# Moving four groups of on-chip tiles to 96 bytes past a multiple of 128

## The chip, the cores and the metric

The kernel runs on one core of a Trainium2 chip. The metric is the time of one execution on the device in microseconds; a kernel's time is the median of its runs. TensorE (PE) multiplies matrices out of the on-chip memory SBUF into PSUM, VectorE (DVE), ScalarE (ACT) and GpSimd (POOL) work on elements, SyncE (SP) issues most transfers. SBUF has 128 partitions; a tile takes the same range of bytes in each of them, and its place is the first byte of that range.

## The reference

One inference step of a streaming encoder of two layers, in float32, for 512 new frames of one prompt and 16 frames of each of 8 running streams, 640 frames in all, with a width of 1024:

```python
# layer 0: convolution module, then feed-forward
a, gate = jnp.split(rms_norm(h, g) @ w_pw1 + b_pw1, 2, axis=-1)
glu = a * jax.nn.sigmoid(gate)
y = depthwise_conv(concat(hist, glu), w_dw) + b_dw          # width 31
h = h + jax.nn.silu(layer_norm(y, ln_g, ln_b)) @ w_pw2 + b_pw2
a, b = jnp.split(rms_norm(h, g) @ w_in, 2, axis=-1)          # 1024 -> 2 x 2816
h = h + (jax.nn.silu(a) * b) @ w_out
# layer 1: shared K and V, attention with 16 heads of 64, then feed-forward
k, v = jnp.split(rms_norm(h, norm_kv) @ w_kv, 2, axis=-1)
q = rms_norm(h, norm_attn) @ w_q
h = h + softmax(q @ k.T / 8 + bias) @ v @ w_o                # banded, own cache per stream
h = swiglu_ffn(h, ...)
return rms_norm(h, norm_final), conv buffers, k, v
```

## The kernel before

Activations stand with features on the partitions: a tile holds 128 features, 8 tiles make the width. The 640 frames are the columns, in two groups: group 0 has 256 (all sample frames and the first 128 of the prompt), group 1 has 384 (`GR`).

Every large product is made of three, since an operand is split into a high and a low half that TensorE takes in the type fp32r: `mm3` (lines 157 to 162) issues, for each tile of 128 features, high weights by high activations (L160), low weights by high activations (L161) and high weights by low activations (L162). Each matmul loads its own 128 x 128 stationary tile first (a PEld row of the profile) and then streams 256 or 384 columns. The activations' halves are the tiles `xh` and `xl` (of group 0 and of group 1), the hidden layer of the feed-forward network has both halves in one tile `hid` per group, and the attention output has `ohi` and `olo`. In the V projection the roles are swapped: xh and xl are stationary and the weights stream.

Weights come from memory as `raw`, 1 MB at a time at most (`wsplit`, L124 and L129); ScalarE makes the high half `whi` (L140), VectorE and GpSimd the low half `wlo` (L144). Each of the three has two buffers.

The order of the work is layer 0's convolution module, with group 0 ahead of group 1 by a written plan (`PLAN`); three chunks of layer 0's feed-forward network for group 0 (6 of 22 hidden tiles each), run while VectorE still convolves group 1; the remaining chunk of 4 for both groups; three chunks of 6 for group 1; the attention of 8 pairs of heads, with the projections of the next pair between; and layer 1's feed-forward network for both groups in chunks of 9, 9 and 4. In a chunk, `ffn_in` makes one hidden tile per step (48 matmuls per group: two halves of the gate, 8 tiles, 3 products), and `out_tile` then adds the chunk's share to each of 8 output tiles (3 products for each hidden tile of the chunk: 18, 12 or 27 matmuls). A scheduler places the instructions of each engine in the program by a simulated timeline; SBUF tiles are placed by pools: constants first (`cst`), then the weights (`wp`), then temporary pools, each tile behind the one allocated before it.

So a tile's place follows from the sizes of all tiles ahead of it. `i4` (L341 of the kernel before) is a constant of 128 bytes right ahead of `xh` and `xl`; `t256s` (L578) is the last constant ahead of the weights; `bt` (L596) stands right ahead of `ohi` and `olo`; `KK` (L706) comes behind these.

Of the kernel before, what the change touches and what calls it, by code (L numbers as in the profile page):

```python
# [8 lines left out]
F32 = mybir.dt.float32  # L9
F32R = mybir.dt.float32r  # L10
# [4 lines left out]
P = 128  # L15
# [5 lines left out]
NP = H // 2  # L21
# [19 lines left out]
F1 = ((0, 9), (9, 9), (18, 4))  # L41
FP = (8, 4)
CM = 6
# [11 lines left out]
SSQ = 'avavavav'  # L55
SCUT = 8
CB, QB, KB = 5, 1, 1
OG = (0, 1)
BO = "a0 s0 a1 s1 b0 b1 t0 p0 c0 t1 c1"
BL = "a0 s0 a1 s1 t0 b0 b1 c0 t1 c1 p0"  # L60
FG = (1, 0)
# [10 lines left out]
def tile_trunk(ctx, tc, xT, vecs, hist, w_pw1, w_pw2, w_in0, w_out0, w_in1, w_out1,  # L72
# [3 lines left out]
    cst = ctx.enter_context(tc.tile_pool(name="cst", bufs=1))  # L76
# [8 lines left out]
    def nm(s):  # L85
        uid[0] += 1
        return f"{s}_{uid[0]}"
# [4 lines left out]
    def w2t():  # L92
        return w2.tile([P, 1024], F32, tag="w2", name=nm("w2"))
# [164 lines left out]
    def ffn_in(wsrc, j, xs, hid, jj, groups, pool):  # L258
        wh, wl = wsplit(wsrc[j], 16, P, pool=pool)
        for g in groups:  # L260
            n = GR[g][1]
            ps = []
            for ab in range(2):
                pt = mmt()
                mm3(pt[:, :n], [(wh[:, (ab * 8 + k) * P:(ab * 8 + k + 1) * P],
                                 wl[:, (ab * 8 + k) * P:(ab * 8 + k + 1) * P]) for k in range(KT)],
                    xk(xs[g], range(KT)))
                ps.append(pt[:, :n])
            bc = xs[g][2]
            with tc.high_priority(offset=HP):  # L270
                s = tp.tile([P, 384], F32, tag="t1", name=nm("t1"))
                t = tp.tile([P, 384], F32, tag="t2", name=nm("t2"))
                if bc is None:
                    nc.scalar.activation(out=s[:, :n], in_=ps[0], func=AF.Silu)
                    nc.vector.tensor_tensor(out=t[:, :n], in0=s[:, :n], in1=ps[1], op=ALU.mult)
                else:
                    nc.vector.tensor_tensor(out=s[:, :n], in0=ps[0], in1=bc, op=ALU.mult)  # L277
                    nc.scalar.activation(out=s[:, :n], in_=s[:, :n], func=AF.Silu)  # L278
                    nc.vector.tensor_tensor(out=t[:, :n], in0=ps[1], in1=bc, op=ALU.mult)  # L279
                    nc.vector.tensor_tensor(out=t[:, :n], in0=s[:, :n], in1=t[:, :n], op=ALU.mult)  # L280
                xsplit(t[:, :n], hid[g][0][:, jj, :], hid[g][1][:, jj, :])
# [23 lines left out]
                for m in range(KT):  # L305
                    out_tile(ws[m // mg], ch, (m % mg) * ch, m, g, hid)

    def ffn(pool, w_in, w_out, xs, groups, chunks, pl=0, og=None, cm=CM):
        for j0, ch in chunks:
            hid = {}  # L310
            for g in groups:
                n = GR[g][1]
                t = pool[g].tile([P, 2 * cm * n], F32, tag=f"hid{g}", name=nm("hid"))
                t = t.bitcast(F32R).rearrange("p (s k n) -> p s k n", s=2, k=cm)
                hid[g] = t[:, 0], t[:, 1]
            for jj in range(ch):
                ffn_in(w_in, j0 + jj, xs, hid, jj, groups, pl)
            ffn_out(w_out, j0, ch, hid, og or groups, pl)
# [19 lines left out]
    nc.gpsimd.memset(gs[:, :, 9, 0:14], 0.0)  # L338
    gp = cp.tile([P, KT, GPW], F32, name="gp", tag="gp")
    nc.gpsimd.memset(gp[:, :, HIST + 384:], 0.0)  # L340
    i4 = cst.tile([P, 32], F32, name="i4", tag="i4")  # L341
    nc.gpsimd.tensor_tensor(out=i4, in0=ident[:, 0:32], in1=ident[:, 32:64], op=ALU.add)
    for b in range(2, 4):
        nc.gpsimd.tensor_tensor(out=i4, in0=i4, in1=ident[:, 32 * b:32 * b + 32], op=ALU.add)
# [5 lines left out]
    with tc.high_priority(offset=2 * HP):  # L350
        xs = [rms(0, V_NCONV, SSQ, SCUT, nc.vector), None]
# [151 lines left out]
    chunks = list(FS)  # L503
# [43 lines left out]
    if FC:  # L547
        ffn({0: hp0, 1: hp1}, w_in0, w_out0, {0: xs0, 1: xs1}, (0, 1), FC)
# [4 lines left out]
    xs = [rms_late(0, None), rms_late(1, None)]  # L553
# [9 lines left out]
    ap = at.enter_context(tc.tile_pool(name="ap", bufs=1))  # L563
# [11 lines left out]
    BS = ap.tile([P, 576], F32, name="BS", tag="BS")  # L575
    nc.gpsimd.memset(BS[:, 0:384], 0.0)
    nc.gpsimd.memset(BS[:, 512:576], NEG)
    ts_ = cst.tile([P, NP], F32, name="t256s", tag="t256s")  # L578
    for b in range(4):
        for hh in range(2):  # L580
            r0 = b * 32 + hh * 16
# [2 lines left out]
                                      ap=[[0, 16], [2 * L, NP]]))  # L584

    def bias_load(p):
        for hh in range(2):
            hd = 2 * p + hh
            nc.sync.dma_start(BP[:, hh, 256:512],
                              bass.AP(tensor=rel.tensor, offset=rel.offset + hd * L + 127,  # L590
                                      ap=[[RELW - 1, P], [1, 256]]))
            nc.gpsimd.tensor_scalar(out=BP[:, hh, 256:512], in0=BP[:, hh, 256:512],
                                    scalar1=t256[:, hd:hd + 1], scalar2=8.0,
                                    op0=ALU.subtract, op1=ALU.mult)
            nc.gpsimd.memset(BP[0:64, hh, 448:512], NEG)
        bt = ap.tile([P, 160], F32, tag="bt", name=nm("bt"), bufs=1)  # L596
        for b in range(4):
            nc.sync.dma_start(bt[b * 32:(b + 1) * 32, 0:128],
                              bass.AP(tensor=rel.tensor, offset=rel.offset + 2 * p * L + 127,
                                      ap=[[L, 2], [RELW - 1, 16], [1, 128]]))  # L600
            nc.sync.dma_start(bt[b * 32:(b + 1) * 32, 128:144],
                              bass.AP(tensor=rel.tensor, offset=rel.offset + 2 * p * L + 255,
                                      ap=[[L, 2], [RELW - 1, 16], [1, 16]]))
        nc.gpsimd.tensor_scalar(out=BS[:, 384:512], in0=bt[:, 0:128], scalar1=ts_[:, p:p + 1],
                                scalar2=8.0, op0=ALU.subtract, op1=ALU.mult)
        for b in range(4):
            nc.gpsimd.tensor_scalar(out=BS[b * 32:(b + 1) * 32, 512 + b * 16:528 + b * 16],
                                    in0=bt[b * 32:(b + 1) * 32, 128:144],
                                    scalar1=ts_[b * 32:(b + 1) * 32, p:p + 1],
                                    scalar2=8.0, op0=ALU.subtract, op1=ALU.mult)  # L610
# [72 lines left out]
    def proj_o(r):  # L683
        wh, wl = wsplit(w_o[r], 16, P)
        for g in OG if r == NP // 2 - 1 else (0, 1):
            g0, n = GR[g]
# [10 lines left out]
    def head_a(p, hh):  # L697
        kt, qt = kts[p], qts[p]
        r = slice(hh * DH, hh * DH + DH)
        S = sp.tile([P, 1280], F32, tag="S", name=nm("S"))  # L700
        mx = ap.tile([P, 4], F32, tag="mx", name=nm("mx"), bufs=3)
        sm = ap.tile([P, 4], F32, tag="sm", name=nm("sm"), bufs=3)
        wide = w2t()
        st = w2t()
        ro = slice(DH - hh * DH, 2 * DH - hh * DH)
        KK = ap.tile([P, 512], F32R, tag="KK", name=nm("KK"), bufs=KB)  # L706
        KL = ap.tile([P, 512], F32R, tag="KL", name=nm("KL"), bufs=KB)
        QQ = ap.tile([P, 512], F32R, tag="QQ", name=nm("QQ"), bufs=KB)
        nc.scalar.activation(out=KK[r], in_=kt[r, P:], func=AF.Copy)
        nc.scalar.activation(out=QQ[r], in_=qt[r, P:], func=AF.Copy)  # L710
        nc.gpsimd.tensor_copy(KK[ro], KK[r].bitcast(F32))
        for to in (r, ro):
            nc.vector.tensor_tensor(out=KL[to], in0=kt[r, P:], in1=KK[r].bitcast(F32),
                                    op=ALU.subtract)
        nc.vector.tensor_tensor(out=QQ[ro], in0=qt[r, P:], in1=QQ[r].bitcast(F32),
                                op=ALU.subtract)
        pss = []
        for i in ORD:
            n = (i + 1) * P
            o = SOFF[i]  # L720
            q = slice(i * P, (i + 1) * P)
            ps = st[:, 640:896] if i == 1 else wide[:, o:o + n]
            nc.tensor.matmul(ps, QQ[:, q], KK[:, 0:n], start=True, stop=False)  # L723
            nc.tensor.matmul(ps, QQ[:, q], KL[:, 0:n], start=False, stop=True)
            pss.append(ps)
        for ii, i in enumerate(ORD):
            n = (i + 1) * P
            o = SOFF[i]
            addmax(S[:, o:o + n], pss[ii], BP[:, hh, 512 - n:512], mx[:, ii:ii + 1])
        rs = softmax_rows(S, mx, sm, [(SOFF[i], (i + 1) * P) for i in ORD])  # L730
        for ii, i in enumerate(ORD):
            n = (i + 1) * P
            o = SOFF[i]
            nc.vector.tensor_scalar(out=S[:, o:o + n], in0=S[:, o:o + n],
                                    scalar1=rs[:, ii:ii + 1], scalar2=None, op0=ALU.mult)
        return S, st
# [128 lines left out]
    tp = hf.enter_context(tc.tile_pool(name="tp1", bufs=2))  # L865
    hpf = hf.enter_context(tc.tile_pool(name="hpf1", bufs=1))
    xs = {g: rms_late(g, V_NFFN + KT) for g in FG}
    ffn({0: hpf, 1: hpf}, w_in1, w_out1, xs, FG, F1, 0, (1, 0), max(ch for _, ch in F1))
    bcs = {}
    with tc.high_priority(offset=HP):  # L870
        for g in (1, 0):
# [4 lines left out]
    for g in (1, 0):  # L876
        g0, n = GR[g]
# [95 lines left out]
```

## Time and profile before

| | us |
|---|---|
| median of 3 runs | 1594.21 |
| lowest and highest run | 1593.93, 1598.01 |
| span of the profiled execution, first to last instruction | 1590.2 |
| TensorE busy in it | 1519.2 |
| VectorE busy in it | 969.4 |
| ScalarE busy in it | 604.7 |
| GpSimd busy in it | 398.0 |

The profiled execution has no time of its own beside its span; the median of the runs is 4.0 us above that span, which is what lies ahead of the first and behind the last instruction, and the difference between executions.

In the profile's rows a line such as L160 is a line of the kernel, an arrow points from the operands to the result, and "128x384" is the shape that streams. A matmul's duration runs until its result is out, and the next begins long before that, so the distance between two starts is what a matmul costs the span. The clock that TensorE was granted was full in nearly all of the span (mean 0.990).

### The profile page before, as it was taken

The numbers are of one execution on the slowest core, as the hardware profiler recorded it, in microseconds if no ns is written. First come the engines' busy times: TensorE is split into PE (matmuls) and PEld (weight loads), VectorE is DVE, ScalarE is ACT, GpSimd is POOL, SyncE is SP. The second block draws the span as 40 slices with busy tenths as digits, with TensorE's granted clock in tenths as the row PEclk, the third lists the DMA queues.
The fourth block names the chain that finished last, engine by engine and source line by source line (L and its number), as shares of the span: only waits on it lengthen the run. The fifth ranks groups of instructions, "written<-read, shape, count | busy, mean of one in ns | idle before, by whom it ended". The sixth has DMA issues, their size and how long they took to land.

```text
span 1590.2 us, 26820 instructions
## 1 busy us (share of the span) xinstructions
PE 1519.2 (96%) x10998; PEld 1450.4 (91%) x10998; DVE 969.4 (61%) x1781; ACT 604.7 (38%) x1064; POOL 398.0 (25%) x368
## 2 busy tenths in 40 slices
PE   5988998989999999999999999998999999999997
PEld 5868898889999999999987898986999999999997
DVE  5995999988535545446776668577544334433335
ACT  4544454535423323234654345443422112221222
POOL 6854577877401000004221111012100000000001
PEclk9999999999999999999999999999999999999999
DMA  7884345444321343434555454451121232112311
GB/s 240 234 221 135 124 127 166 133 160 159 133 80 59 115 146 102 136 113 139 211 180 171 168 191 160 159 169 52 56 80 45 60 121 80 56 43 76 107 54 67
DMA packets 58700, 199.98 MB, mean 126 GB/s; under 512 B 10193, under 2 KB 22737, under 8 KB 45777
## 3 DMA queue, kind: packets, MB, share of 16 engines
q1 hardware_dynamic: 58288, 197.96, 38.5%
q8 instruction: 86, 1.41, 0.4%
q10 hardware_dynamic: 288, 0.31, 0.1%
q14 instruction: 38, 0.30, 0.1%
HBM read 187.02 MB, written 11.22 MB: 125 GB/s over the span
## 4 chain that ended last, share of the span: by engine, by line
PE 74%; DVE 15%; issue 3%; POOL 3%; DMA 3%; ACT 2%; SPq 0%; POOLq 0%; ACTq 0%; DVEq 0%
PE mm L160 22%; PE mm L162 22%; PE mm L161 22%; DVE w L424 5%; DVE wlo L144 4%; DVE xl L150 2%; PE w L779 1%; PE am L764 1%; PE am L747 1%; PE am L810 1%; ACT whi L140 1%; DVE hid L150 1%; DMA x<-sc 1%; POOL wlo L144 1%; PE w L723 1%
## 5 line engine op out<-in xcount | busy, mean ns | idle before, releaser
L161 PE MATMUL mm<-xh,wlo 128*128 128x256 f32 (+1 forms) x2048 | 638.8, 313 | 13.1 <-DVE wlo L144 12.5
L160 PE MATMUL mm<-xh,whi 128*128 128x256 f32 (+1 forms) x2048 | 635.9, 314 | 7.9 <-ACT xh L149 3.6
L162 PE MATMUL mm<-xl,whi 128*128 128x256 f32 (+1 forms) x2048 | 634.8, 312 | 0.3
L161 PEld LDWEIGHTS mm<-xh,wlo 128*128 128x128 f32 x2048 | 387.9, 190 | 16.6 <-DVE wlo L144 15.6
L160 PEld LDWEIGHTS mm<-xh,whi 128*128 128x128 f32 x2048 | 385.9, 190 | 13.1 <-ACT xh L149 6.7
L162 PEld LDWEIGHTS mm<-xl,whi 128*128 128x128 f32 x2048 | 387.1, 190 | 2.5 <-DVE xl L150 1.4
L140 ACT ACTIVATE whi<-raw 128x2048 fp32r<-128x2048 f32 (+3 forms) x140 | 235.0, 1682 | 340.3 <-PE mm L162 284.0
L144 DVE TENSOR_TENSOR wlo<-raw,whi 128x2048 fp32r<-128x2048 f32 (+6 forms) x140 | 259.7, 1857 | 77.9 <-ACT whi L140 76.3
L161 PE MATMUL mm<-hid,wlo 128*128 128x384 f32 (+1 forms) x704 | 217.3, 310 | 6.6 <-DVE wlo L144 6.6
L162 PE MATMUL mm<-hid,whi 128*128 128x384 f32 (+1 forms) x704 | 215.1, 309 | 0.0
L160 PE MATMUL mm<-hid,whi 128*128 128x384 f32 (+1 forms) x704 | 213.8, 309 | 0.0
L144 POOL TENSOR_TENSOR wlo<-raw,whi 128x1536 fp32r<-128x1536 f32 (+3 forms) x50 | 145.1, 2905 | 69.5 <-ACT whi L140 68.6
L279 DVE TENSOR_TENSOR t<-mm,bc 128x384 f32<-128x384 f32 x66 | 33.8, 512 | 194.5 <-PE mm L162 194.5
L161 PEld LDWEIGHTS mm<-hid,wlo 128*128 128x128 f32 x704 | 132.3, 188 | 8.0 <-DVE wlo L144 8.0
L162 PEld LDWEIGHTS mm<-hid,whi 128*128 128x128 f32 x704 | 131.9, 188 | 0.4 <-DVE hid L150 0.3
L160 PEld LDWEIGHTS mm<-hid,whi 128*128 128x128 f32 x704 | 131.4, 188 | 0.3 <-ACT hid L149 0.2
L217 POOL TENSOR_TENSOR rst<-rst,mhalf 128x2 f32<-128x2 f32 (+1 forms) x7 | 6.0, 863 | 460.2 <-DVE rst L213 460.2
L290 DVE TENSOR_TENSOR h<-mm,h 128x384 f32<-128x384 f32 (+1 forms) x112 | 53.9, 486 | 107.3 <-PE mm L162 107.2
L424 DVE SCALAR_TENSOR_TENSOR w<-gp,dwv,w 128x384 f32<-128x384 f32 x180 | 103.9, 611 | 0.8
L278 ACT ACTIVATE t<-t 128x384 f32<-128x384 f32 x66 | 32.3, 489 | 162.3 <-DVE t L277 162.3
L149 ACT ACTIVATE hid<-t 128x384 fp32r<-128x384 f32 (+1 forms) x88 | 40.6, 462 | 119.1 <-DVE t L280 85.4
L183 POOL TENSOR_TENSOR acc<-sq,sq 128x384 f32<-128x384 f32 (+1 forms) x9 | 9.2, 1023 | 265.2 <-ACT sq L167 265.1
(154 smaller groups left out, 1897.3 us busy)
## 6 DMA issues: line engine op xcount, KB each, us to landing
raw<-in_w_in SPq DMA_DIRECT2D x62, 1024.0 KB
raw<-in_w_pw SPq DMA_DIRECT2D x22, 1024.0 KB
raw<-in_w_out SPq DMA_DIRECT2D x24, 768.0 KB
cache<-in_ck SPq DMA_DIRECT2D x32, 512.0 KB
cache<-in_cv SPq DMA_DIRECT2D x32, 512.0 KB
raw<-in_w_out SPq DMA_DIRECT2D x16, 576.0 KB
raw<-in_w_kq SPq DMA_DIRECT2D x8, 1024.0 KB
x<-sc SPq DMA_DIRECT2D x16, 368.0 KB
```

The lines of the kernel that those rows point to most:

```text
L140: nc.scalar.activation(out=hi[:, a:b], in_=raw[:, a:b], func=AF.Copy)
L144: eng.tensor_tensor(out=lo[:, a:b], in0=raw[:, a:b], in1=hi[:, a:b].bitcast(F32), op=ALU.subtract)
L149: nc.scalar.activation(out=hi, in_=src, func=AF.Copy)
L150: nc.vector.tensor_tensor(out=lo, in0=src, in1=hi.bitcast(F32), op=ALU.subtract)
L160: nc.tensor.matmul(ps, wh, xh, start=(i == 0), stop=False)
L161: nc.tensor.matmul(ps, wl, xh, start=False, stop=False)
L162: nc.tensor.matmul(ps, wh, xl, start=False, stop=(i == last))
L278: nc.scalar.activation(out=s[:, :n], in_=s[:, :n], func=AF.Silu)
L279: nc.vector.tensor_tensor(out=t[:, :n], in0=ps[1], in1=bc, op=ALU.mult)
L290: nc.vector.tensor_tensor(out=hp(g, m), in0=pt[:, :n], in1=hp(g, m), op=ALU.add)
L424: nc.vector.scalar_tensor_tensor(out=dst, in0=src, scalar=wj, in1=dst, op0=ALU.mult, op1=ALU.add)
L723: nc.tensor.matmul(ps, QQ[:, q], KK[:, 0:n], start=True, stop=False)
```

## The change

Four constants are added, and five places use them. Tiles are made larger than what is used of them, so that what is allocated behind them, or the used part itself, moves:

- `i4` gets 24 more float32 (96 bytes) behind it: all later constants move by 96 bytes, xh and xl of both groups among them.
- `t256s` gets 8 more (32 bytes): with the 96 this makes 128, so that weights and all later tiles move by 128.
- `bt` gets 16 more (64 bytes): `ohi` and `olo` and what lies behind them move by 192 in all.
- `KK` gets 16 more ahead of its used part, which brings it and what is behind it to 256.
- Layer 1's hidden tile of group 1 gets 16 more ahead of its used part.

The two built programs give these places, as bytes past a multiple of 128 (in brackets the place modulo 512):

| tile | before | after |
|---|---|---|
| xh, xl (group 0 and group 1) | 0 (256) | 96 (352) |
| raw, whi, wlo (both buffers) | 32 (416) | 32 (32) |
| hid of layer 0, both groups | 96 (96) | 96 (224) |
| hid of layer 1, group 0 | 32 (32) | 32 (160) |
| hid of layer 1, group 1 | 32 (32) | 96 (224) |
| ohi, olo (pairs 0 to 6) | 32 | 96 |
| KK, KL, QQ | 96 | 96 |
| the factors bc of group 1, of group 0 | 32, 64 | 0, 32 |

All rows inside these tiles have lengths that are multiples of 128 bytes. The instructions, their order on every engine and their waits are the same in both programs.

```diff
+XPAD, WPAD, OPAD, HPAD = 24, 8, 16, 16
...
-    def ffn(pool, w_in, w_out, xs, groups, chunks, pl=0, og=None, cm=CM):
+    def ffn(pool, w_in, w_out, xs, groups, chunks, pl=0, og=None, cm=CM, pad=(0, 0)):
...
-                t = pool[g].tile([P, 2 * cm * n], F32, tag=f"hid{g}", name=nm("hid"))
-                t = t.bitcast(F32R).rearrange("p (s k n) -> p s k n", s=2, k=cm)
+                t = pool[g].tile([P, pad[g] + 2 * cm * n], F32, tag=f"hid{g}", name=nm("hid"))
+                t = t[:, pad[g]:].bitcast(F32R).rearrange("p (s k n) -> p s k n", s=2, k=cm)
...
-    i4 = cst.tile([P, 32], F32, name="i4", tag="i4")
+    i4 = cst.tile([P, 32 + XPAD], F32, name="i4", tag="i4")[:, 0:32]
...
-    ts_ = cst.tile([P, NP], F32, name="t256s", tag="t256s")
+    ts_ = cst.tile([P, NP + WPAD], F32, name="t256s", tag="t256s")[:, 0:NP]
...
-        bt = ap.tile([P, 160], F32, tag="bt", name=nm("bt"), bufs=1)
+        bt = ap.tile([P, 160 + OPAD], F32, tag="bt", name=nm("bt"), bufs=1)
...
-        KK = ap.tile([P, 512], F32R, tag="KK", name=nm("KK"), bufs=KB)
+        KK = ap.tile([P, OPAD + 512], F32R, tag="KK", name=nm("KK"), bufs=KB)[:, OPAD:]
...
-    ffn({0: hpf, 1: hpf}, w_in1, w_out1, xs, FG, F1, 0, (1, 0), max(ch for _, ch in F1))
+    ffn({0: hpf, 1: hpf}, w_in1, w_out1, xs, FG, F1, 0, (1, 0), max(ch for _, ch in F1), (0, HPAD))
```

## The prediction

> **What bounds the kernel now.** I read the page's head and its first part, then the busy time by stage, then the waits of TensorE, and last single matmuls in the timeline, since the change alters nothing but where tiles lie. TensorE first:
>
> ```profile
> span 1590.2 us, 26820 instructions
> PE 1519.2 (96%) x10998; PEld 1450.4 (91%) x10998; DVE 969.4 (61%) x1781; ACT 604.7 (38%) x1064; POOL 398.0 (25%) x368
> ```
>
> The share hides two regimes. By stage (TensorE alone, columns: window, its length, busy time and instructions, granted clock, DMA share, GB/s):
>
> ```profile
> 0.00:389.00 389.00, 339.07 (x2652) 0.97 0.55 170
> 389.00:757.00 368.00, 366.57 (x2218) 1.00 0.36 116
> 757.00:1116.00 359.00, 348.98 (x2986) 1.00 0.48 160
> 1116.00:1577.00 461.00, 461.00 (x3128) 1.00 0.21 67
> ```
>
> From 389 us TensorE is idle for 1.4 us, then 10.0, then 0.0: whatever shortens its stream there shortens the span. Before 389 us it loses 50 us. The last such stretch, the first feed-forward chunks of group 0, with all engines, and its one cause of waiting:
>
> ```profile
> 206.00:389.00 183.00, 165.15 (x1324) 160.22 (x1324) 170.84 (x256) 91.71 (x122) 147.97 (x74) 0.98 0.46 150
> ...
> PE mm L161 <- DVE wlo L144: 17.5, 15, 3.6
> ```
>
> VectorE (fourth group of figures) is busy 170.84 of 183 us and TensorE waits 17.5 us for its low halves of the weights; a quicker matmul there mostly waits longer.
>
> What a matmul costs is its start-to-start time, the **pace**, not its duration, since they overlap. These rows of the timeline are the first matmuls of stretches that have no gap:
>
> ```profile
> 638.26 0.34 PE L160 MATMUL mm<-hid,whi 128*128 128x384 f32 x1
> ...
> 663.22 0.34 PE L160 MATMUL mm<-xh,whi 128*128 128x384 f32 x1
> ...
> 714.10 0.34 PE L160 MATMUL mm<-hid,whi 128*128 128x384 f32 x1
> ...
> 1549.00 0.34 PE L160 MATMUL mm<-hid,whi 128*128 128x384 f32 x1
> ...
> 1565.90 0.28 PE L160 MATMUL mm<-hid,whi 128*128 128x256 f32 x1
> ```
>
> From 638.26 to 663.22 us run 8 output tiles of 6 x 3 matmuls of layer 0: 24.96 us / 144 = **173.3 ns**. From 663.22 to 714.10 run 6 weight steps of 48 on xh and xl: 50.88 / 288 = **176.7**. From 1549.00 to 1565.90 run 8 x 4 x 3 of layer 1: 16.90 / 96 = **176.0**. Engine, shape and operation are the same, and the runs are long. What differs is the place. By the built programs (the table ahead) the weights lie 32 bytes past a multiple of 128 throughout; layer 0's hid lies at 96 (64 from the weights), layer 1's at 32 (0 from them), xh and xl at 0. The same for 256 columns:
>
> ```profile
> 369.91 0.28 PE L160 MATMUL mm<-hid,whi 128*128 128x256 f32 x1
> ...
> 373.32 0.39 PE L160 MATMUL mm<-hid,whi 128*128 128x256 f32 x2
> ...
> 482.29 0.28 PE L160 MATMUL mm<-hid,whi 128*128 128x256 f32 x1
> ...
> 493.60 0.34 PE L160 MATMUL mm<-hid,whi 128*128 128x384 f32 x1
> ...
> 510.37 0.33 PE L160 MATMUL mm<-xh,whi 128*128 128x384 f32 x1
> ...
> 1145.44 0.28 PE L160 MATMUL mm<-xh,whi 128*128 128x256 f32 x1
> ...
> 1151.20 0.34 PE L160 MATMUL mm<-xh,whi 128*128 128x384 f32 x1
> ```
>
> hid at 96: 30 matmuls from 369.91 to 373.32 are **113.7 ns** each, 96 from 482.29 to 493.60 are **117.8**; xh at 0, 48 from 1145.44 to 1151.20: **120.0**. And 96 of 384 columns from 493.60 to 510.37: **174.7**. So a place at 96 has a faster and a slower pattern, and each observed one is faster than xh. One stretch of layer 0 (561 to 587 us, 144 matmuls), interrupted by small matmuls, is worse:
>
> ```profile
> L162 PE MATMUL mm<-hid,whi 128*128 128x384 f32 x20 | 6.8, 338 | 0.0
> ...
> L160 PE MATMUL mm<-hid,whi 128*128 128x384 f32 x43 | 13.9, 335 | 0.0
> ```
>
> Its mean duration is 338 ns (first row, 576 to 586 us) against 335 in the fast stretch (second row, 640 to 662 us). Durations move with the pace, so I take 173.3 + 3 = 176.3 ns for all of it, a little pessimistic for its start.
>
> **The change part by part.** No instruction is added, removed or reordered on any engine. xh and xl of both groups go from 0 to 96, layer 1's hid of group 1 from 32 to 96, the attention outputs from 32 to 96; weights stay at 32, layer 0's hid at 96, and layer 1's hid of group 0 at 32. The counts after 389 us:
>
> ```profile
> L161 PE MATMUL mm<-xh,wlo 128*128 128x384 f32 x896 | 303.7, 339 | 0.0
> ...
> L161 PE MATMUL mm<-xh,wlo 128*128 128x256 f32 x544 | 153.7, 283 | 0.0
> ...
> L162 PE MATMUL mm<-wlo,xh 128*128 128x256 f32 x160 | 45.3, 283 | 0.0
> ...
> L161 PE MATMUL mm<-ohi,wlo 128*128 128x384 f32 x64 | 21.6, 337 | 0.0
> ...
> L161 PE MATMUL mm<-ohi,wlo 128*128 128x256 f32 x64 | 18.1, 284 | 0.0
> ...
> L160 PE MATMUL mm<-hid,whi 128*128 128x384 f32 x176 | 59.5, 338 | 0.0
> ```
>
> Each row is one of three products, so there are 2688 matmuls of 384 columns and 1632 of 256 on xh and xl, 480 of the V projection (weights moving, xh stationary), 192 and 192 on the attention output, and 528 on layer 1's hid of group 1 (last row, from 1100 us on).
>
> The new pace is the mean of what the trace shows at 96. 384 columns: (288 x 173.3 + 96 x 174.7 + 144 x 176.3) / 528 = **174.4**. 256 columns: three chunks like 113.7 and one like 117.8 give **114.7**.
>
> - xh and xl, 384: 2688 x (176.7 - 174.4) = 6.2 us (at best x 3.4 = 9.1, at worst x 0.4 = 1.1).
> - xh and xl, 256: 1632 x (120.0 - 114.7) = 8.6 (x 6.3 = 10.3; x 2.2 = 3.6).
> - layer 1's hid, 384: 528 x (176.0 - 174.4) = 0.8 (1.4; 0).
> - attention output: durations 337 and 284 are those of layer 1's hid and of xh, so 192 x 1.6 + 192 x 5.3 = 1.3 (1.7; 0.4).
> - V projection: moving and stationary swap roles; the two go from 32 apart to 64 apart. No row shows that pair at 64. Between nothing and 480 x (120.0 - 114.7) = 2.5 I take 0.7, nearer nothing, as its duration (283) is that of xh.
> - before 389 us: 1440 matmuls of 256 and 384 of 384 would give 1440 x 6.3 + 384 x 3.4 = 10.4 at best, nothing if VectorE decides throughout. I take 1.0, since VectorE does in the stretch above.
>
> Sum: 6.2 + 8.6 + 0.8 + 1.3 + 0.7 + 1.0 = 18.6 us. The span becomes 1590.2 - 18.6 = 1571.6; the median of the runs, 1594.21, lies 4.0 us above the span before, which gives **1576 us**.
>
> Other engines touch the moved tiles too:
>
> ```profile
> L149 ACT ACTIVATE hid<-t 128x384 fp32r<-128x384 f32 x19 | 9.6, 507 | 0.0
> ...
> L149 ACT ACTIVATE hid<-t 128x384 fp32r<-128x384 f32 x22 | 11.6, 525 | 85.4 <-DVE t L280 85.4
> ```
>
> ScalarE's write of hid takes 507 ns in layer 0 (at 96) and 525 in layer 1 (at 32): 18 ns either way, under 14 us of TensorE work per step of both groups. I cost it at nothing; uncovered, 22 writes would be 0.4 us. Nothing that feeds TensorE becomes late: from 1116 to 1577 us it never waits, and its steps would shorten by some 3% only.
>
> A rule of the Trainium skill speaks against all this. "TensorE: Matmul & The Clock Gate", section "Step-by-step: what each phase is for", says that the moving operand and the weights come through two independent read ports, so that loading the next weights takes no bandwidth from the running matmul. By that rule a tile's place would have no price. The rows of 335 against 339 ns for the same form at the same clock do not fit, unless something other than the place makes them.
>
> **The rivals.**
>
> - *Nothing changes.* The paces come from what ran before a stretch, not from the place. For it: hid at the same place ran with 335 and with 338. Against it: 96 matmuls of layer 1's hid in one run stayed at 176.0, and xh, entered from everything, stays at 120.0 and 176.7. Time 1594.
> - *The slower pattern takes over.* Every tile at 96 settles at 117.8 and 176.3: 1.1 + 3.6 + 0 + 0.4 = 5.1 us, 1589. For it: once in a pattern a stretch keeps it. Against it: half of the 384 work and most of the 256 work at 96 were in the fast one.
> - *The new place of xh is a bad one.* Modulo 256, layer 0's hid lies 192 past the weights, but xh will lie 64 past them, which no row shows. If the order of the two matters, the moving read can collide at each step. Price: each matmul takes the longest duration that xh rows show in an undisturbed stretch, 342 instead of 339 and 286 instead of 283:
>
> ```profile
> L160 PE MATMUL mm<-xh,whi x94: 337/338/342, 588.1 to 637.7; 128*128 128x384 f32 x94
> ...
> L160 PE MATMUL mm<-xh,whi x13: 279/279/286, 1131.6 to 1135.9; 128*128 128x256 f32 x13
> ```
>
>   (2688 + 1632) x 3 ns = 13 us more, 1607. It decides as soon as the xh rows pass 339 and 283.
>
> **How the numbers follow.** A measurement of this kernel tells 0.3%, 4.8 us, from no change. Chances: forecast 0.77, slower pattern throughout 0.07 (0.3% faster, on the bound, so split), nothing 0.08, bad place 0.08. Faster 0.80, same 0.12, slower 0.08. The forecast's own ends: all fast gives 9.1 + 10.3 + 1.4 + 1.7 + 2.5 = 25.0, and 35.4 with all of the early part, 1559; I leave out half of that early part: 1564. Upwards the range takes in the slower pattern: 1590.
>
> **What would show it.** Right: xh of 384 columns at 335 to 337 ns instead of 339, of 256 columns at 276 to 281 instead of 283, layer 1's hid of group 1 at 335 to 336 while that of group 0 does not move; the stretch from the first wait-free matmul of layer 1 to its last shorter by about 2%; VectorE wlo waits before 389 us larger. Wrong: xh rows unchanged at 339 and 283 (places do not matter), or above them; or the xh rows shorter and TensorE idle after 389 us.

## The result, and the profile after

The changed kernel takes **1577.26 us** (median of 4 runs, 1574.62 to 1581.78), the kernel before 1594.07 beside it: a ratio of **0.9886**, 95% interval 0.9867 to 0.9905, or 16.8 us. The forecast was 1576.

The profiled execution of the change was the slowest of its four runs (1581.78; its span is 1580.0), so the two profiled spans differ by only 10.2 us. The page of the change begins:

```profile
span 1580.0 us, 26820 instructions
PE 1506.5 (95%) x10998; PEld 1435.8 (91%) x10998; DVE 970.0 (61%) x1781; ACT 604.6 (38%) x1064; POOL 398.1 (25%) x368
```

The counts are those of before on every engine; TensorE alone is busy for 12.7 us less. Where the time went is best read between landmarks that both traces have, the starts of single matmuls. Each column gives how many microseconds shorter the piece is than in the profiled execution before (negative: longer); e2 to e9 are the experiments below.

| piece, and its length before | change | e2 | e3 | e4 | e6b | e7 | e9 |
|---|---|---|---|---|---|---|---|
| first matmul to the first 384-column hid of layer 0, 480.7 | -0.3 | 1.6 | 1.4 | 2.5 | 4.8 | 3.1 | 4.5 |
| to the last hid of layer 0, 245.3 | 2.5 | 2.5 | 0.0 | 2.5 | 3.2 | 3.1 | 3.2 |
| to the last attention-output matmul, 364.5 | 0.5 | 0.2 | -2.5 | 0.8 | 2.8 | -1.0 | 3.1 |
| to the first 384-column hid of layer 1, 133.3 | 1.1 | 1.1 | -1.3 | 1.0 | 3.7 | 2.7 | 2.7 |
| to the last one of layer 1, 329.1 | 6.6 | 3.5 | 3.2 | 6.6 | 6.2 | 5.4 | 9.9 |
| to the last matmul, 17.6 | 0.0 | 0.0 | 0.3 | 0.1 | 0.0 | -0.1 | 0.1 |

In the change most of the gain is in layer 1's feed-forward network. In this execution the start gained nothing. These are the stretch 206 to 389 us (all engines) and its one large wait, as they were shown of before:

```profile
206.00:389.00 183.00, 163.82 (x1293) 159.24 (x1292) 168.53 (x249) 88.61 (x117) 146.38 (x73) 0.95 0.46 146
...
PE mm L162 <- DVE wlo L145: 18.6, 16, 3.6
```

TensorE's wait for VectorE's low halves grew from 17.5 to 18.6 us (one line further down in the changed kernel). The granted clock in this stretch (the figure after the busy times) was 0.95 against 0.98 before, so the start is not a fair comparison: the matmul that starts at 389 us before comes 1.7 us later in this execution, while in e2 and e4, with xh at the same distance and a clock of 0.97, it comes 0.3 and 0.9 us earlier. (Both programs issue the same 10998 matmuls in the same order, so each has its counterpart.) At the end of the attention, too, the change's execution ran at a lower clock. TensorE alone from 1070 to 1120 us, first before, then the change (the column after the busy time is the granted clock):

```profile
1070.00:1120.00 50.00, 42.58 (x333) 1.00 0.12 43
```

```profile
1070.00:1120.00 50.00, 42.59 (x309) 0.90 0.13 43
```

The busy time is the same, but a tenth of the clock is missing for 50 us: up to 5.0 us of work. From the matmul that starts at 1070 us before to the one that starts at 1120, the change takes 4.1 us longer. The same window stood at 0.90 in the profiled executions of e2, e3 and e7, which lose 3.8, 3.9 and 4.1 us there, at 0.97 in e4 and e9, which lose 1.2 and 1.1, and at 1.00 in e6b, which loses nothing. In these single executions it goes with no edit that was tried; why it falls is not shown. With these 4.1 us and the 1.7 of the start the profiled execution's gain of 10.2 becomes 16.0, close to the 16.8 of the medians. In the table the first row and the two rows around the end of the attention are to be read with that in mind.

The paces, first in layer 0 (timeline of the change, the first matmul of each stretch, as in the prediction):

```profile
482.69 0.28 PE L161 MATMUL mm<-hid,whi 128*128 128x256 f32 x1
...
493.99 0.34 PE L161 MATMUL mm<-hid,whi 128*128 128x384 f32 x1
...
510.95 0.34 PE L161 MATMUL mm<-xh,whi 128*128 128x384 f32 x1
...
636.74 0.34 PE L161 MATMUL mm<-hid,whi 128*128 128x384 f32 x1
...
661.89 0.34 PE L161 MATMUL mm<-xh,whi 128*128 128x384 f32 x1
...
711.81 0.34 PE L161 MATMUL mm<-hid,whi 128*128 128x384 f32 x1
```

xh and xl: (711.81 - 661.89) / 288 = **173.3 ns** where before had 176.7. But layer 0's hid, whose distance from the weights did not change, got slower: 144 from 636.74 to 661.89 are 174.7 where they were 173.3, and 96 from 493.99 to 510.95 are 176.7 where they were 174.7. The 96 of 256 columns before them stay at (493.99 - 482.69) / 96 = 117.7. Now layer 1:

```profile
1213.35 0.28 PE L161 MATMUL mm<-xh,whi 128*128 128x256 f32 x1
...
1219.00 0.34 PE L161 MATMUL mm<-xh,whi 128*128 128x384 f32 x1
...
1227.32 0.28 PE L161 MATMUL mm<-xh,whi 128*128 128x256 f32 x1
...
1245.51 0.28 PE L161 MATMUL mm<-hid,whi 128*128 128x256 f32 x1
...
1248.57 0.33 PE L161 MATMUL mm<-hid,whi 128*128 128x384 f32 x1
...
1253.24 0.28 PE L161 MATMUL mm<-hid,whi 128*128 128x256 f32 x1
...
1538.70 0.34 PE L161 MATMUL mm<-hid,whi 128*128 128x384 f32 x1
...
1555.66 0.28 PE L161 MATMUL mm<-hid,whi 128*128 128x256 f32 x1
```

48 of xh with 256 columns take 5.65 us, **117.7 ns** (120.0 before); 48 with 384 columns 8.32, 173.3. 27 of hid of group 0 take 3.06, **113.3**; 27 of group 1 take 4.67, **173.0**. The last chunk is different at the same place: 96 of group 1 from 1538.70 are 176.7. What runs ahead of them is xh of group 0, and not hid. The mean over all of layer 1 (groups by shape, from 1110 us; mean ns is the last number before the idle time):

```profile
L162 PE MATMUL mm<-xh,wlo 128*128 128x384 f32 x343 | 115.3, 336 | 0.0
...
L161 PE MATMUL mm<-xh,whi 128*128 128x256 f32 x352 | 98.0, 279 | 0.0
...
L162 PE MATMUL mm<-hid,wlo 128*128 128x384 f32 x176 | 59.1, 336 | 0.0
...
L162 PE MATMUL mm<-hid,wlo 128*128 128x256 f32 x172 | 47.7, 278 | 0.0
```

The last row is hid with 256 columns, group 0. Before, its row had 282 ns:

```profile
L161 PE MATMUL mm<-hid,wlo 128*128 128x256 f32 x172 | 48.5, 282 | 0.0
```

**A row of the table of places ahead is wrong.** It lets layer 1's hid of group 0 stay at 32 (160). In the built program this tile lies *behind* that of group 1, so the 64 bytes put into group 1's tile push it too: it is at 96 (224). The prediction's statement that this tile "does not move" rests on that row, and so do the places that the expectations of e3 and e4 give for it.

**Distances.** From here on a place is counted as the distance of the moving operand past the weights, modulo 256 bytes, because that is what the experiments find to matter:

| moving operand | before | change |
|---|---|---|
| xh, xl | 96 | 64 |
| hid of layer 0 | 192 | 192 |
| hid of layer 1, both groups | 128 | 192 |
| ohi, olo, pairs 0 to 6 | 128 | 192 |

### The profile page after: what moved, and what is told of

Same layout as the page of the kernel before. It is cut to its first block, busy times and chain, and to the rows that moved or that the text cites. A ratio compares the mean times of both kernels' runs of the same rounds, so it can differ in the third digit from the quotient of the medians.

```text
span 1580.0 us, 26820 instructions
## 1 busy us (share of the span) xinstructions
PE 1506.5 (95%) x10998; PEld 1435.8 (91%) x10998; DVE 970.0 (61%) x1781; ACT 604.6 (38%) x1064; POOL 398.1 (25%) x368
## 4 chain that ended last, share of the span: by engine, by line
PE 74%; DVE 15%; DMA 3%; ACT 3%; issue 2%; POOL 2%; SPq 0%; POOLq 0%; ACTq 0%; DVEq 0%
PE mm L161 22%; PE mm L163 22%; PE mm L162 22%; DVE w L425 5%; DVE wlo L145 4%; PE w L780 1%; DMA x<-sc 1%; DVE xl L151 1%; PE am L765 1%; PE am L748 1%; PE am L811 1%; ACT whi L141 1%; DVE hid L151 1%; DMA raw<-in_w_pw 1%; PE w L724 1%
## 5 line engine op out<-in xcount | busy, mean ns | idle before, releaser
L162 PEld LDWEIGHTS mm<-xh,wlo 128*128 128x128 f32 x2048 | 390.3, 191 | 17.5 <-DVE wlo L145 16.5
```

Source lines behind the costliest of these rows:

```text
L162: nc.tensor.matmul(ps, wl, xh, start=False, stop=False)
```

## The experiments

**e1: the place alone.** No network, only the three products of `mm3` on fixed operands, 72 in a row per stretch, for 4 places of the weights and 8 of the moving operand; the list is run forward and then backward.

```diff
+    combos = [(wp, xp, n) for wp in WPL for xp in XPL for n in (384, 256)]
+    for c in combos + combos[::-1]:
+        pt = stretch(*c)      # 3 tiles of 8 x (whi,xh; wlo,xh; whi,xl)
```

> This kernel leaves out everything but matmuls: one pair of weight halves and one pair of activation halves, each with spare columns, so that a view of them can begin at any place; stretches of 72 matmuls (3 output tiles of 8 x 3 products) for each of 4 places of the weights (0, 32, 64, 160 modulo 256), 8 places of the moving operand (0 to 224 in steps of 32) and 384 or 256 columns, once in this order and once in reverse. Theory A (distance): the pace depends on the place of the moving operand minus that of the weights modulo 128 alone: 64 apart gives 173 to 175 ns and 113 to 118, 0 apart 176 and 118.5, 96 apart 176.7 and 120. Theory B (own place): it depends on the place of the moving operand alone, 96 being the best for every place of the weights. Theory C (history): the same pair has another pace in the reverse pass, as different as pairs are from each other.

Five neighbouring stretches in the timeline, weights at 32: moving operand at 96 with 384 and 256 columns, at 128 with both, then at 160:

```profile
81.20 0.34 PE L117 MATMUL mm<-xh,whi 128*128 128x384 f32 x1
...
93.68 0.28 PE L117 MATMUL mm<-xh,whi 128*128 128x256 f32 x1
...
102.16 0.34 PE L117 MATMUL mm<-xh,whi 128*128 128x384 f32 x1
...
114.88 0.28 PE L117 MATMUL mm<-xh,whi 128*128 128x256 f32 x1
...
123.52 0.34 PE L117 MATMUL mm<-xh,whi 128*128 128x384 f32 x1
```

At distance 64: 12.48 / 72 = 173.3 ns and 8.48 / 72 = 117.8. At distance 96: 12.72 / 72 = 176.7 and 8.64 / 72 = 120.0. No other engine does anything here. All stretches, from the starts of the second half of each (where the two directions differ, both values):

| distance mod 256 | 0 | 32 | 64 | 96 | 128 | 160 | 192 | 224 |
|---|---|---|---|---|---|---|---|---|
| 384 columns, ns | 173.3 | 173.3 / 176.7 | 173.3 | 176.7 | 176.1 | 173.3 | 173.3 / 176.7 | 173.3 |
| 256 columns, ns | 120.0 | 116.7 | 117.8 | 120.0 | 118.6 | 118.7 / 117.4 | 113.3 / 117.8 | 118.3 |

Where two values stand, 384 columns at 32 and 256 columns at 160 and 192 go with the direction of the list, that is with what ran before. Weights at 64, whose list starts elsewhere, depart from the other three at 160 and 192, and the 176.7 of 384 columns at 192 is theirs alone, in the forward pass. Otherwise the four weight places give the same rows, so only the difference of the two places counts, besides what ran before. These rows reproduce before (96: 176.7 and 120.0; layer 1's hid at 128: 176.0) and the xh of the change (64: 173.3 and 117.7). Distances 0 and 128, or 64 and 192, are not alike, and places 32 bytes below the weights give the row of those 224 above: the modulus is 256, not the 128 of theory A. Distance 96, where xh lay, is the only one that is always at the highest value for both widths.

**e2 and e3: the parts of the change apart.** e2 moves xh, xl and the weights as the change does and leaves layer 1's hid and the attention outputs at distance 128. e3 does the opposite; xh stays at distance 96.

```diff
-XPAD, WPAD, OPAD, HPAD = 24, 8, 16, 16
+XPAD, WPAD, OPAD, HPAD = 24, 8, 0, 0     # e2
+XPAD, WPAD, OPAD, HPAD = 0, 0, 16, 16    # e3
```

> Only xh and xl are moved (and all later tiles by 128 bytes, which keeps their place modulo 128); the padding ahead of the attention outputs and of layer 1's hidden tile is left out. By the sum of the prediction 16.5 of 18.6 us come from here: 0.8% to 1.2% faster than before, 1576 to 1581 us, xh rows as in the changed kernel (335 and 281 ns), layer 1's hid of group 1 still at 338. If the hidden tiles' pace depends only on what runs ahead of them, their rows fall to 335 here too, although their place is unchanged.

> Only the attention outputs and layer 1's hidden tile of group 1 are moved to 96; xh, xl and the weights stay. By the sum 2.1 us: about 1592 us, hid of group 1 in layer 1 at 335 to 336 ns instead of 338, that of group 0 at 281 as before, xh at 339 and 283. If the neighbour's place decides (group 0 and group 1 alternate there), hid of group 0 falls to 276 as it does in the changed kernel, though its own place is kept; if xh decides by what it leaves behind, neither falls.

e2: 1583.15 us against 1593.53, ratio 0.9939 (0.9924 to 0.9954): 10.4 us, so xh and xl are the larger part, but less than the expected 1576 to 1581. Its hid of layer 1 stays at 176.0 and 118.8 ns in the mean, as before. e3, one run: 1590.89 beside 1593.53. In its landmarks layer 1 gains 3.2 us, while attention and the way to layer 1 lost 3.8; that is the stretch with the clock of 0.90, which lost 3.9. Layer 1's hid in e3 (timeline):

```profile
1243.74 0.28 PE L161 MATMUL mm<-hid,whi 128*128 128x256 f32 x1
...
1246.92 0.34 PE L161 MATMUL mm<-hid,whi 128*128 128x384 f32 x1
...
1251.60 0.28 PE L161 MATMUL mm<-hid,whi 128*128 128x256 f32 x1
...
1254.66 0.33 PE L161 MATMUL mm<-hid,whi 128*128 128x384 f32 x1
```

The first 27 of group 0 in the chunk take 3.18 / 27 = 117.8 ns; from the next round on they fall to 3.06 / 27 = 113.3, and 27 of group 1 to 4.68 / 27 = 173.3. Both tiles are at distance 192 here; what looked at first like a neighbour's effect on a tile that had not moved is its real place.

**e4: every place 96 bytes lower, every distance as in the change.**

```diff
-XPAD, WPAD, OPAD, HPAD = 24, 8, 16, 16
+XPAD, WPAD, OPAD, HPAD = 0, 8, 16, 16
```

> The distances of the changed kernel with other places: xh and xl stay at 0, the weights and all later tiles go 32 bytes further (weights at 64, layer 0's hid at 0, layer 1's hid at 64 for group 0 and 0 for group 1, attention outputs at 0). Theory A (distance): as the changed kernel, 1574 to 1580 us, xh rows 335 and 281 ns. Theory B (own place 96 is what is good): no tile lies at 96 any more, so no faster than before, 1592 us or more, xh rows 339 and 283.

1578.15 us (1577.43 to 1580.95), ratio 0.9913 (0.9895 to 0.9932), which overlaps that of the change. The paces of the long stretches are the same to 0.1 ns, the ones that got slower included (layer 0's hid 176.67 and 174.68 in both). Where the tiles lie in the memory doesn't count; how far they are apart does. The words "96 bytes past a multiple of 128" describe what the change does, not why it works.

**e5: pairs of places.** As e1, with weights at 32, but 48 matmuls of 384 columns alternate with 48 of 256, for all 8 x 8 pairs of distances, since the kernel alternates its two groups.

```diff
+    for xp1 in XPL:
+        for xp0 in XPL:
+            for _ in range(2):
+                stretch(WPL[0], xp1, 384, 2)
+                pt = stretch(WPL[0], xp0, 256, 2)
```

> As the first table (matmuls alone, the rest of the computation left out), with the weights at 32, but stretches of 48 matmuls of 384 columns and of 48 of 256 columns alternate, as in the steps that serve both groups; each of 8 places for the wide operand with each of 8 for the narrow one, two rounds of the pair each, of which the second is read. Theory D (distance modulo 256, found in the first table): each form keeps the pace that it had alone, 173.3 except 176.7 at a distance of 96 and 176.0 at 128, and 116.7 to 120.0. Theory E (distance and what ran before): the pace of one form changes with the place of the other; above all the narrow form at a distance of 128 falls from 118.6 to 113.5 where the wide one lies at 192, as in layer 1 of the changed kernel.

From the starts of the second pair of stretches: 384 columns keep 176.5 to 176.7 ns at 96 and 175.9 to 176.1 at 128 whatever the other width does, and 173.3 to 173.9 at 0 and 64. 256 columns keep 119.6 to 119.9 at 0 and 119.8 to 120.1 at 96. But at 64 and at 192 the 256-column rows have two values, 117.7 to 117.9 and 113.3 to 113.8, and they go with the place of the 384 columns ahead of them. The sign that theory E named above all does not come: 256 columns at 128 behind 384 at 192 stay at 118.5; the row of the change that suggested it was hid of group 0, which lay at 192 and not at 128. Sums of both widths, the place of the 384 columns first: before (96, 96) 296.7, the worst of all 64; the change (64, 64) 291.1; (192, 192) 288.4; best (224, 64) and (0, 192), 286.8.

**e6: xh at 192 by one number.** Only the weights move, by 160 bytes, and with them everything behind; xh and xl come to distance 192, all other distances stay as before.

```diff
-XPAD, WPAD, OPAD, HPAD = 24, 8, 16, 16
+XPAD, WPAD, OPAD, HPAD = 0, 40, 0, 0
```

> xh and xl stay, the weights and all later tiles go 160 bytes further: xh and xl lie 192 past the weights modulo 256, where layer 0's hidden tile lay in the trace of before; all other distances are those of the kernel before. If distance counts modulo 128, this is as good as the kernel with xh and xl alone moved to 64: 1583 us, xh rows 335 and 281 ns. If it counts modulo 256, the rows differ from those: 384 columns between 335 and 338 ns, 256 columns 276 or 281. Both at the fast end would be 2688 x 3.3 + 1632 x 6.5 = 19 us less than before, 1574; both at the slow end 4 us less, 1590.

> The kernel with xh and xl at 192 once more, for its single matmuls. Theory E: by the table of pairs 192 and 192 give 174.7 and 113.7 ns, so rows of about 336 and 276 ns for xh where both groups alternate, and 1573 to 1575 us. Theory D: 173.3 to 176.7 and 113.3 to 117.8.

1573.86 us (four executions of 1573.08 to 1575.45), ratio 0.9877 (0.986 to 0.9893). A fifth execution, the one that was profiled, took 3199 us and is left out; why it did is not known. e6b is the same kernel profiled once more (1571.38). There xh and xl run at 173.3 and **113.4** ns (e5 had 174.7 and 113.7 for this pair), and layer 0's hid, again not moved, goes to 173.3 and 113.4 as well. Layer 1's hid stays at 175.9 to 176.2 and 118.4 to 118.7. One padding of 160 bytes gives what the five of the change give; the intervals overlap.

**e7: the best pairs of e5, a miss.** xh of group 1 at 224, of group 0 at 64; layer 1's hid was meant to lie at 0 for group 1 and 192 for group 0.

```diff
-XPAD, WPAD, OPAD, HPAD = 24, 8, 16, 16
+X0PAD, WPAD, OPAD, HPAD = 24, 8, 16, 16
...
-    ffn({0: hpf, 1: hpf}, w_in1, w_out1, xs, FG, F1, 0, (1, 0), max(ch for _, ch in F1), (0, HPAD))
+    ffn({0: hpf, 1: hpf}, w_in1, w_out1, xs, FG, F1, 0, (1, 0), max(ch for _, ch in F1), (HPAD, HPAD))
```

> Places chosen from the table of pairs: xh and xl of group 1 lie 224 past the weights modulo 256, of group 0 64 past them; layer 0's hid of group 1 and layer 1's hid of group 1 at 0, layer 1's hid of group 0 at 192, attention outputs at 192. Theory E (distance modulo 256 and what ran before): the pair 224 and 64 takes 173.4 and 113.4 ns against 173.3 and 117.7 for the changed kernel's 64 and 64, so 1632 x 4.3 = 7.0 us on the narrow form, 528 x 1.7 = 0.9 on layer 0's hid, about 1 on layer 1's hid and 1 on the V projection: some 10 us less than the changed kernel, 1566 to 1570 us, 0.982 to 0.986 of the time before. Theory D (distance modulo 256 alone): the narrow form at 64 keeps 117.8, so 1574 to 1578.

1578.75 us, ratio 0.9902 (0.9883 to 0.9921). xh and hid of layer 1 in its timeline:

```profile
1223.34 0.28 PE L167 MATMUL mm<-xh,whi 128*128 128x256 f32 x1
...
1228.78 0.34 PE L167 MATMUL mm<-hid,whi 128*128 128x384 f32 x1
...
1233.50 0.28 PE L167 MATMUL mm<-hid,whi 128*128 128x256 f32 x1
...
1236.73 0.34 PE L167 MATMUL mm<-hid,whi 128*128 128x384 f32 x1
...
1241.51 0.28 PE L167 MATMUL mm<-hid,whi 128*128 128x256 f32 x1
```

xh does what e5 and theory E say: 5.44 / 48 = 113.3 ns, not the 117.8 of theory D. hid doesn't: 27 of 256 columns take 3.23 us, 119.6, and 27 of 384 take 4.78, 177.0. The reason is the order of the two tiles again: group 1's lies first, so the built program has group 1 at 192 and group 0 at 0, and e5's pair (192, 0) is 176.9 and 119.6. The table held in layer 1; the tile was put in the wrong place. In the means of layer 1 that costs 528 x (120.1 - 114.6) + 528 x (176.4 - 174.2) = 4.1 us against the change. The time is above both forecasts, and the rest of the 10 us that theory E expected is not accounted for.

**e9: every hid, xh, xl and attention output at 192.** e6's weights with the change's paddings for hid and the attention output.

```diff
-XPAD, WPAD, OPAD, HPAD = 24, 8, 16, 16
+XPAD, WPAD, OPAD, HPAD = 0, 40, 16, 16
```

> Everything that moves past the weights in the two feed-forward networks now lies 192 bytes past them modulo 256: xh and xl, layer 0's hid, both hid tiles of layer 1, ohi and olo of pairs 0 to 6. Theory (the pace is set by the distance of the moving operand from the weights modulo 256): xh and xl stay at 173.3 and 113.4 ns as in e6b, layer 1's hid falls from 176.0 and 118.5 to 173.2 and 113.5. From the 1573.9 us of e6_x192 that takes 528 x 2.8 = 1.5, 528 x 5.0 = 2.6 and about 0.7 for the attention output: 1569 us. Rival (at 192 there are two patterns, and which one a stretch falls into is not set by the place alone): layer 1's hid runs at 176.7 and 117.8, which is worth 528 x (-0.7 + 0.7) = nothing against e6: 1573 us. Nothing but xh and xl counts: 1574 us.

**1568.46 us** (1566.22 to 1573.88), where the theory had 1569; ratio **0.984** (0.9817 to 0.9862), an interval just below that of the change. Its page and its timeline, in layer 0 and in layer 1:

```profile
span 1566.7 us, 26820 instructions
PE 1491.2 (95%) x10998; PEld 1422.1 (91%) x10998; DVE 970.1 (62%) x1781; ACT 604.8 (39%) x1064; POOL 397.3 (25%) x368
```

```profile
478.18 0.28 PE L161 MATMUL mm<-hid,whi 128*128 128x256 f32 x1
...
489.06 0.33 PE L161 MATMUL mm<-hid,whi 128*128 128x384 f32 x1
...
505.70 0.34 PE L161 MATMUL mm<-xh,whi 128*128 128x384 f32 x1
...
1203.87 0.28 PE L161 MATMUL mm<-xh,whi 128*128 128x256 f32 x1
...
1209.31 0.33 PE L161 MATMUL mm<-xh,whi 128*128 128x384 f32 x1
...
1217.63 0.28 PE L161 MATMUL mm<-xh,whi 128*128 128x256 f32 x1
...
1227.75 0.28 PE L161 MATMUL mm<-hid,whi 128*128 128x256 f32 x1
...
1230.81 0.33 PE L161 MATMUL mm<-hid,whi 128*128 128x384 f32 x1
...
1235.49 0.28 PE L161 MATMUL mm<-hid,whi 128*128 128x256 f32 x1
```

In each of these stretches both widths are at the lowest values of all the tables: 10.88 / 96 = 113.3 and 16.64 / 96 = 173.3 for hid of layer 0, 5.44 / 48 = 113.3 and 8.32 / 48 = 173.3 for xh, 3.06 / 27 = 113.3 and 4.68 / 27 = 173.3 for hid of layer 1.

**e11 and e12: the distance from which weights? Not settled.** Two weights A and B, 64 (in e11 also 128) bytes apart, alternate with two moving operands x1 and x2, in stretches of 48 matmuls, so that each matmul has one distance from its own weights and another from those that are loaded next. e12 runs e11's first half forward, backward and forward.

```diff
+                nc.tensor.matmul(pt[:, :n], whi[:, w1 + k * P:w1 + (k + 1) * P],
+                                 xh[:, x1 + k * n:x1 + (k + 1) * n], start=(k == 0), stop=False)
+                nc.tensor.matmul(pt[:, :n], wlo[:, w2 + k * P:w2 + (k + 1) * P],
+                                 xl[:, x2 + k * n:x2 + (k + 1) * n], start=False, stop=(k == KT - 1))
...
+    for c in combos:                                # e11
+    for c in combos + combos[::-1] + combos:        # e12
```

> Matmuls alone, nothing of the network: stretches of 48, in which a matmul with weights A (at 32) moving x1 and one with weights B (64 or 128 bytes further) moving x2 alternate, for all 8 x 8 places of x1 and x2 and for 256 and 384 columns. Each matmul so has one distance from its own weights and another from the weights that are loaded while it runs, the next one's. Theory 'next' (the moving read collides with the load of the following weights): the mean pace of a stretch goes by (x1 - B) and (x2 - A). Theory 'own': by (x1 - A) and (x2 - B). With B 64 bytes past A and 256 columns, by the table of e1 (32: 116.7, 96: 120.0, 160: about 118): x1, x2 at 96 from their own weights are 32 and 160 from the next; 'own' gives 120.0 and 'next' 117.4; x1, x2 at 96 from the next weights are 160 and 32 from their own; 'own' gives 117.4 and 'next' 120.0. For 384 columns 176.7 against 173.3 in the same way. A third way, that the distance between x1 and x2 (between one moving operand and the next) counts, gives stretches that depend on x1 - x2 alone, and the same table for both B.

> Matmuls alone, nothing of the network, as in e11: stretches of 48 in which two weights 64 bytes apart alternate, with all 8 x 8 places of the two moving operands and 256 and 384 columns; but the list of 128 stretches is run three times, forward, backward and forward, so that each stretch is entered from another neighbour in the second pass. In e11 the paces fell on a few levels (116.7, 118.3 and 120.0 ns; 173.3, 175.0 and 176.7) and neither the own nor the next weights' distance explained which. If the two places set the pace all the same, in a way that one distance does not describe, the three passes agree within 0.5 ns in at least 9 of 10 stretches, and with e11. If the state that a stretch is entered with sets the pace where places alternate, the passes differ by 1.5 ns or more in at least a third of the stretches, even the first and the third.

e11: neither. With B 64 past A and 256 columns, x1 and x2 at 96 from their own weights gave 120.0 ns, at 96 from the next weights also 120.0; with 384 columns 176.7 and 176.7. A sum of one term for each of the two distances accounts for at most 0.38 of the variance of a table, by either reading, and the distance between x1 and x2 for less than 0.2. e12: in the two forward passes all 126 stretches (the first of each width left out, as the run's first matmuls start 213 ns apart) agree within 0.5 ns, and with e11. The backward pass differs from them by 0.5 ns or more in 14% of the stretches of 256 columns and in 17% of those of 384 (by 1.5 or more in 8% and 14%). So neither expectation is met in full: with the same places in the same order the paces repeat, and in about one stretch of six what ran before has a say. What it is in a distance that slows a matmul stays open.

## Why the prediction was right, step by step

**What bounds the kernel: right.** The gain came where TensorE never waits: layer 1's feed-forward network, first hid to last, is shorter by 6.6 of 329.1 us, 2.0%, as forecast. Before 389 us little was gained: the matmul there comes 0.3 and 0.9 us earlier in e2 and e4, and 1.3 in e3, where xh did not move.

**The sum: near, by errors that cancel.** Measured terms are the forecast's counts times the change of the mean pace (starts less than 260 ns apart, after 389 us) between the two profiled executions.

| term | forecast | measured | pace, ns |
|---|---|---|---|
| xh, xl, 384 columns | 6.2 | 2688 x 3.0 = 8.1 | 176.9 to 173.9 |
| xh, xl, 256 columns | 8.6 | 1632 x 2.2 = 3.6 | 121.4 to 119.2 |
| layer 1's hid, group 1 | 0.8 | 528 x 1.9 = 1.0 | 176.1 to 174.2 |
| layer 1's hid, group 0 | none | 528 x 4.3 = 2.3 | 118.9 to 114.6 |
| layer 0's hid, 384 columns | none | 528 x -1.1 = -0.6 | 174.1 to 175.2 |
| attention output | 1.3 | 192 x 1.5 + 192 x 2.1 = 0.7 | 177.9 to 176.4; 131.6 to 129.5 |
| V projection | 0.7 | 480 x 2.5 = 1.2 | 121.8 to 119.3 |
| before 389 us | 1.0 | -1.7, in e2 and e4 0.3 and 0.9 | |
| sum | 18.6 | 16.3 without the last | medians: 16.8 |

Matmul by matmul, from 389 us on and without the stretch from 1070 to 1120, the change gains 16.1 us.

- *The step that failed* is "The new pace is the mean of what the trace shows at 96". It counted places modulo 128, and all rows "at 96" were layer 0's hid, at distance 192 modulo 256. xh went to 64. e1 has a steady 173.3 there for 384 columns, better than the mean of 174.4, and a steady 117.8 for 256, worse than 114.7 (e5 has 113.3 for 256 at the same distance as well, behind some places of the 384 columns). The third rival saw that 64 and 192 might differ and priced the difference only as a collision; its 1607 did not happen. Had layer 0's hid and the new xh been compared modulo 256, the honest bound for both widths would have been "no row shows this place".
- *Group 0's hid of layer 1* was left out because of the wrong row of the table of places. It is worth more than the term of group 1.
- *Layer 0's hid costs 0.6 us more in its long stretches at an unchanged distance* (0.2 with the interrupted stretch, matmul by matmul). The prediction took "a faster and a slower pattern" at its place as a given mixture. In the runs the pattern goes with the place of xh, whose matmuls run ahead. With xh at 96 (before, e3) hid of layer 0 ran at 117.8, 174.7 and 173.3 ns in its long stretches (96 of 256 columns, 96 of 384, twice 144 of 384); with xh at 64 (change, e2, e4) at 117.8, 176.7 and 174.7; with xh at 192 (e6b, e9) at 113.4, 173.3 and 173.3. The same values to 0.1 ns in each group. The last chunk of layer 1 shows it once more: 96 of hid with 384 columns at 192, behind xh of group 0, take 174.7 with xh at 96 (e3), 176.7 at 64 (change) and 173.3 at 192 (e9).
- *The attention output* gained about half of its term: the price had been that of xh.

**The signs it named.** xh of 384 columns was to fall to 335 to 337 ns: 336 in layer 1. Of 256 columns to 276 to 281: 279. hid of group 1 to 335 to 336: 336. hid of group 0 was not to move: 282 to 278, for the reason above. The wait for wlo was to grow: 17.5 to 18.6 us in the change, 18.8 in e2, 19.7 in e9; 17.2 in e3, where xh did not move.

**The rivals.** "Nothing changes" fell with e1, e4 and the result. "The slower pattern takes over" was right for 256 columns of xh, which run at the slower 117.8 and gain 3.6 us, what this rival gave them, but wrong for 384 columns, which run at 173.3. A stretch does keep the pattern it enters with (the last chunk's 176.7). By the Trainium skill, "TensorE: Matmul & The Clock Gate", section "Step-by-step: what each phase is for", weights and moving operand come through independent read ports, which would leave a place without a price. The trace doesn't agree: in e1 the same matmuls at the same clock, with no other engine at work, take 173.3 or 176.7 ns and 113.3 to 120.0 ns by nothing but their places and, at some distances, what ran before.

## What to carry to other kernels

Where TensorE streams matmuls that each load their own weights, and nothing else is waited for, take the start-to-start time of long stretches from the trace and set it beside the distance of the moving operand from the weights; here 192 bytes modulo 256 for every operand (e9) was worth 1.6%, by paddings that cost no instruction. Judge a place in the order of the kernel, since the pace at 192 went with the place of the tile that ran ahead. Read the places from the built program, each tile for itself, since a padding moves every tile behind it: one wrong row cost this study a term of its forecast and one experiment its point. Rows at one place say nothing about another that only looks alike by a modulus nobody has measured.

## What was not expected of the hardware

- The pace depends on the distance of two operands in the memory modulo 256 bytes, by up to 2% (173.3 to 176.7 ns, 384 columns) and 6% (113.3 to 120.0, 256 columns), with TensorE alone at work.
- It is not a function of that distance alone. At 192 the same stretch takes 113.4 or 117.8 ns, by what ran before it, and keeps this for as long as it runs (96 matmuls in the change). In repeated passes of the same sequence the paces return within 0.5 ns.
- The granted clock at the end of the attention was between 0.90 and 1.00 in executions of kernels with the same instructions, and the executions at 0.90 lost about 4 us there; its cause was not looked for.
- Why a distance is slow is not shown. e11 speaks against the distance from the own or from the next weights alone: where the two differ, neither orders the paces.
